# Two transformer blocks on one core: the first layer's modulation sums as one-column matrix products, and its first norm tile by tile

## The chip, the cores and the metric

One core of one Trainium2 chip runs the whole program in a single launch. The metric is device time in microseconds (us); smaller is better. TensorE is called PE, its weight loads PEld, VectorE DVE, ScalarE ACT, GpSimd POOL; SP is the engine that only issues DMAs.

## The reference

A batch of one, 512 tokens of width 1024, fp32. Two layers form a first block, two hybrid layers a second one. The change lies in the first layer of the first block, and there in the adaptive modulation and in the first norm:

```python
s_lat, s_ctx = silu(c), silu(c_ctx)
mod_l = split(s_lat @ ada_w[i] + ada_b[i], 6)      # shift, scale, gate for mixer and for MLP
a_lat = rmsnorm(h_lat, norm1_g[i]) * (1 + mod_l[1]) + mod_l[0]
a_ctx = ...the same for 256 context tokens, with s_ctx...
p_lat = a_lat @ mix_w_in + mix_b_in                # q, k, v and three Hyena streams
kv_ctx = a_ctx @ mix_w_in[:, kv] + mix_b_in[kv]
# differential attention (4 heads, two softmaxes each), a long convolution beside it,
# an output projection, then h_lat + mod_l[2] * y and an MLP with mod_l[3:6]
```

Each of the six modulation vectors of a layer is a vector of 1024 times a 1024 x 1024 matrix. The kernel treats them as twelve halves of 512 columns: halves 0 and 1 are the first shift, 2 and 3 the first scale, 4 to 11 the rest.

## The kernel before

**Products.** Activations lie with channels on the partitions. Every fp32 operand is split into a high part (a rounded copy by ACT) and a low part (source minus high, by DVE or POOL), and a product is three matrix products: high by high, low by high, high by low (`mm3`, lines 458 to 460). A product of 1024 channels is 8 such triples into one of six PSUM banks (`ps`). Two more banks (`pss`) serve everything small: broadcasts, transposes of the attention weights, filter products, statistics.

**The stream of weights.** `plan` writes the order of all weight pieces by hand. Each piece is 512 KB and lands in one of six raw buffers; SP issues the piece that is six later when a buffer's readers are done (`_done_part`). `prefetch` walks ahead of the consumer: high parts for one piece more than low parts. Modulation pieces ("ada") stand between weight pieces and are worked off when the walk passes them. In the first layer the order is: halves 0 and 1 (pieces 0 to 7), q (8), four pieces of k (9 to 12), then pairs of "qh" pieces with two or four ada pieces after each pair.

**Modulation sums before.** A half is four pieces, each 256 rows by 512 columns. `_ada_step` multiplies each row block by its scalar and adds it to an accumulator: in mode `G` by a POOL multiply (line 371) and a POOL add (line 383), in mode `A` by an ACT multiply (line 373) and a POOL add, in mode `V` by one DVE instruction (line 378). A half takes 8 multiplies and 7 adds of 128 x 512. DVE then transposes and reduces the accumulator (lines 416 and 418), and a selection product and a DVE add finish it. The string `ada='GGAGGA'` gives the modes of halves 4 to 9. `first_shift` does the same for halves 0 and 1 with two vectors (latent and context), modes `fs='GGVA'`, and sums over partitions by 32 products with a column of ones (line 1101). `v_shift` sums the shift times the v weights, one accumulator on DVE, one on ACT and POOL (`vs='VA'`).

**The start.** For k from 0 to 7 a strip product (line 1012, 8 products of two columns) gives the scale, `inputs(k)` makes the split operands and the squares, and `groups(k)` runs 18 large products of the v projection. Beside them run the Hyena filter's hidden layer, the first filter taps (line 872) and `first_shift` by the counts in `fstep`. After group 7 the reciprocal root is broadcast by PE (line 563) and copied by ACT to SBUF, the ones products run, then DVE multiplies all eight x tiles (line 1117), and per tile ACT makes the high part, POOL or DVE a full copy (line 1127), DVE or POOL the low part (line 1121). The same follows for the context (lines 1138 to 1141). Then come the projections q, k (four, each also for the context), and 16 attention steps. A step runs the scores (1497, 1498), softmax, one qh projection as filler (`gemm1`), transposes into `pss` (1538), splits of them (1550) and the product with v.

Of the kernel before, what the change touches and what calls it, by code (L numbers as in the profile page):

```python
# [19 lines left out]
T = 512  # L20
TC = 256
# [4 lines left out]
RAW_BUFS = 6  # L26
# [24 lines left out]
def r(t):  # L51
    return t.bitcast(F32R)


class Weights:
# [9 lines left out]


PR = dict(
    l_q='G',
    l_k='V',
    l_qh='V',  # L70
    l_mo='G',
# [29 lines left out]
    ax='VVVGVVVV',  # L101
    al='VGVVVVGV',
    at='GGGGVGGG',
# [32 lines left out]
class Prog:  # L136
    def __init__(self, tc, ctx, a, out, tap=None):
# [21 lines left out]
        self.ada_acc = {}  # L159
        self.ada_late, self.ada_mode = [], "G"  # L160
        self.look = LOOK
        self.l_eng = self.V
        self.cnt = {}
        self.past0 = False
# [94 lines left out]
    def _emit_l(self):  # L259
        p, part = self.parts[self.cur_l]  # L260
        self.cur_l += 1
        kind, extra = part
        if kind == "ada":
            self._ada_step(p, *extra)
            self._done_part(p)
        elif kind == "w":
# [108 lines left out]
    def add_scaled(self, mode, out, x, sc):  # L375

        if mode == "V":
            self.V.scalar_tensor_tensor(out, x, sc, out, op0=ALU.mult, op1=ALU.add)
        else:
            t = self.get()  # L380
            v = t[:, 0:x.shape[-1]]
            self.scaled(mode, v, x, sc)
            self.G.tensor_tensor(out, out, v, op=ALU.add)  # L383
            self.put(t)

    def _ada_step(self, p, layer, half, i):
        raw = p["raw"]
# [547 lines left out]

    def first_shift(self):

        for half in range(2):
            acc = [self.get(), self.get()]
            for i in range(4):  # L940
                p = self.parts[self.cur][0]
                self.cur_h = self.cur_l = self.cur = self.cur + 1
                for kk in range(2):
                    k = 2 * i + kk
                    for c, o in enumerate(acc):
                        sc, w = self.s2[:, k, c:c + 1], p["raw"][:, kk, :]
                        if k == 0:
                            self.scaled(PR["fs"][2 * half + c], o[:], w, sc)
                        else:
                            self.add_scaled(PR["fs"][2 * half + c], o[:], w, sc)  # L950
                self._done_part(p)
                if i == 3:
                    self.first_acc.append(acc)
                yield


    SIDE = [7, 0, 9, 0, 0, 0, 0, 0]
# [2 lines left out]
    def start(self):  # L960
# [38 lines left out]
        cx = [cxt[k // 2][:, k % 2 * TC:(k % 2 + 1) * TC] for k in range(8)]  # L999
        self.conv3_setup()  # L1000
        gg, sh = c.tile([128, 8, 2], F32, name="gg"), c.tile([128, 8, 2], F32, name="sh")
        b1 = c.tile([128, 8], F32, name="b1")
# [3 lines left out]
        hidden, shift, self.first_acc = self.hyena_hidden(z, w1, w2, w3), self.first_shift(), []  # L1006

        def strip(k):

# [52 lines left out]
        for k in range(8):  # L1062
# [19 lines left out]
            if k == 6:  # L1082
# [11 lines left out]
        bp, rc = self.bcast(y[:, 4:6], 2, self.ps_s, "pss"), self.get()  # L1094
        S.copy(rc[:, 0:TC], bp[:, 0:TC])
        ps = self.ps_s.tile([128, 512], F32, tag="pss", name="pss")
        for half, acc in enumerate(self.first_acc):
            for c_, o in enumerate(acc):
                for k in range(4):
                    j = 8 * c_ + 4 * half + k  # L1100
                    PE.matmul(ps[:, j:j + 1], lhsT=o[:, k * 128:(k + 1) * 128], rhs=self.ones[:, 0:1], start=True, stop=True)
            self.put(acc)
        for c_ in range(2):
            V.tensor_tensor(sh[:, :, c_], ps[:, 8 * c_:8 * c_ + 8], self.col("ada_b", 0, 8), op=ALU.add)
        self.vt = []

        def out(i):
            t = self.get()
            S.activation(t[:], pss[i][:], AF.Copy, scale=y[:, i:i + 1])
            self.vt.append(t)  # L1110

        for i in range(2):
            out(i)
        A, AC = [], []
        self.l_eng = G
        for k in range(8):
            self.eng("ax").tensor_tensor(xs[k][:], xs[k][:], rb[:], op=ALU.mult)
        self.prefetch(2)

        def low(t, hl):  # L1120
            self.eng("al").tensor_tensor(r(hl[1])[:], t[:], hl[0][:], op=ALU.subtract)
            self.put(t)

        for k in range(8):
            t, hl = self.get(), self.pair()
            S.activation(r(hl[0])[:], xs[k][:], AF.Identity, scale=gg[:, k, 0:1], bias=sh[:, k, 0:1])
            self.eng("at").tensor_scalar(t[:], xs[k][:], gg[:, k, 0:1], sh[:, k, 0:1], op0=ALU.mult, op1=ALU.add)
            A.append(hl)
            self.put(xs[k])
            low(t, hl)  # L1130
        self.put(rb)
        for i in range(2, 6):
            out(i)
        for _ in range(8 - 2 * len(PR["tapk"])):
            next(self.filt)
        for k in range(8):
            t, p = self.get(), self.get()
            self.eng("cx").tensor_tensor(cx[k], cx[k], rc[:, 0:TC], op=ALU.mult)
            S.activation(r(p)[:, 0:TC], cx[k], AF.Identity, scale=gg[:, k, 1:2], bias=sh[:, k, 1:2])
            self.eng("ct").tensor_scalar(t[:, 0:TC], cx[k], gg[:, k, 1:2], sh[:, k, 1:2], op0=ALU.mult, op1=ALU.add)  # L1140
            self.eng("cl").tensor_tensor(r(p)[:, TC:2 * TC], t[:, 0:TC], p[:, 0:TC], op=ALU.subtract)
            AC.append(p)
            self.put(t)
        self.put(rc)
        self.sh = sh
        self.put(cxt)
        next(self.filt)
        self.vw = vw
        return A, AC

# [48 lines left out]
    def layer0(self):  # L1199
# [10 lines left out]
        def gemm1(label):  # L1210
            return self.gemm1(label, axs)
# [3 lines left out]
        def zq(j, ps):  # L1215
            a = self.rope(ps, bin_(j), rope)
            self.defer(lambda: Q.__setitem__(j, self.stack_put(a, True)), PR["zqd"])

        zq(0, gemm1("q"))
        self.l_eng = V  # L1220
        KL, KC = [], []
        for j in range(4):
            w = self.consume("k")
            ps, pc = self.ps(), self.ps()
            for k in range(8):
                self.mm3(ps[:], w[k], axs[k], k == 0, k == 7)
# [1188 lines left out]
```

## Time and profile before

| | us |
|---|---|
| median of 3 runs | 2660.74 |
| lowest, highest | 2656.87, 2663.26 |
| the profiled execution | 2662.61 |
| its span, first to last instruction | 2660.8 |

Mean granted PE clock 0.955 of full. Busy over the span: PE 2477.6, PEld 2066.3, DVE 1831.9, POOL 1458.0, ACT 1136.4 us. The mixer of the changed layer takes about the first 466 us. An engine's busy time counts the time in which some instruction of it is under way; for PE, ends are modelled, so a busy PE is not a PE at its peak. The time of a wait stands in square brackets in a timeline, with the instruction that ended it.

### The profile page before, as it was taken

How to read it: one execution, taken by the hardware profiler on the slowest of the kernel's cores; microseconds unless marked ns; L12 is line 12 of the kernel's file. 1: busy time of each engine (PE TensorE's matmuls, PEld its weight loads, DVE VectorE, ACT ScalarE, POOL GpSimd, SP SyncE). 2: the span in 40 equal slices, each digit the busy share in tenths (PEclk: the TensorE clock that was granted, in tenths of full speed). 3: DMA queues.
4: the chain of work that ended last, by engine and by line, in shares of the span. 5: the costliest groups of instructions: out<-in, count | busy, mean ns of one | idle time of the engine just before them, and what ended most of it. 6: DMA issues, size and time to landing. Idle time of an engine off the chain costs nothing.

```text
span 2660.8 us, 31920 instructions
## 1 busy us (share of the span) xinstructions
PE 2477.6 (93%) x11472; PEld 2066.3 (78%) x11472; DVE 1831.9 (69%) x2646; ACT 1136.4 (43%) x2105; POOL 1458.0 (55%) x1168
## 2 busy tenths in 40 slices
PE   7787878999989899999879999999999899999998
PEld 6565767887868788888768888888887688888887
DVE  7899987776666787766778677455477876733334
ACT  3446653532233543334567545222256654522231
POOL 6687756399991379963575346878136744100001
PEclk8798888999999999999989999999999899999999
DMA  7233322366664167762212235666332123233321
GB/s 253 73 125 96 118 88 80 97 193 200 197 204 140 48 171 213 218 188 82 89 52 70 72 116 164 184 195 199 111 89 87 44 82 119 81 94 97 101 86 50
DMA packets 433367, 330.29 MB, mean 124 GB/s; under 512 B 11799, under 2 KB 365207, under 8 KB 433208
## 3 DMA queue, kind: packets, MB, share of 16 engines
q1 hardware_dynamic: 429976, 322.22, 40.4%
q0 software_dynamic: 3232, 6.03, 0.7%
q8 instruction: 90, 1.47, 0.2%
q14 instruction: 69, 0.57, 0.1%
HBM read 319.82 MB, written 8.39 MB: 123 GB/s over the span
## 4 chain that ended last, share of the span: by engine, by line
PE 59%; DVE 19%; POOL 11%; ACT 4%; issue 3%; DMA 2%; SPq 0%; POOLq 0%; DVEq 0%; ACTq 0%
PE ps L458 17%; PE ps L459 16%; PE ps L460 16%; POOL slot L383 6%; POOL slot L371 5%; PE ps L619 4%; PE ps L477 3%; DVE slot L273 2%; DVE slot L1988 1%; DVE slot L527 1%; DVE slot L1940 1%; DVE slot L1550 1%; DVE slot L2053 1%; PE pss L574 1%; PE ps L1382 1%
## 5 line engine op out<-in xcount | busy, mean ns | idle before, releaser
L458 PE MATMUL ps<-slot 128*128 128x512 f32 (+1 forms) x3024 | 1168.7, 386 | 56.8 <-DVE slot L527 17.0
L460 PE MATMUL ps<-slot 128*128 128x512 f32 (+1 forms) x3024 | 1159.3, 383 | 20.8 <-DVE slot L527 9.2
L459 PE MATMUL ps<-slot 128*128 128x512 f32 (+1 forms) x3024 | 1161.0, 384 | 18.4 <-DVE slot L273 15.5
L458 PEld LDWEIGHTS ps<-slot 128*128 128x128 f32 x3024 | 583.4, 193 | 171.5 <-DVE slot L527 20.1
L460 PEld LDWEIGHTS ps<-slot 128*128 128x128 f32 x3024 | 582.3, 193 | 132.0 <-DVE slot L527 9.4
L459 PEld LDWEIGHTS ps<-slot 128*128 128x128 f32 x3024 | 583.4, 193 | 126.3 <-DVE slot L273 18.1
L255 ACT CAST slot<-raw 128x512 fp32r<-128x512 f32 (+1 forms) x764 | 425.7, 612 | 345.0 <-DMA raw<-in_mlp_w_dram 219.4
L273 DVE TENSOR_TENSOR slot<-raw,slot 128x512 fp32r<-128x512 f32 x588 | 510.2, 911 | 35.4 <-ACT slot L255 34.1
L383 POOL TENSOR_TENSOR slot<-slot 128x512 f32<-128x512 f32 x336 | 491.3, 1462 | 59.0 <-ACT slot L373 31.6
L542 POOL TENSOR_TENSOR slot<-slot 128x512 f32<-128x512 f32 (+1 forms) x64 | 90.8, 1423 | 585.5 <-ACT slot L536 585.0
L273 POOL TENSOR_TENSOR slot<-raw,slot 128x512 fp32r<-128x512 f32 (+1 forms) x176 | 251.7, 1454 | 175.8 <-ACT slot L255 134.8
L371 POOL TENSOR_SCALAR slot<-raw,cols 128x512 f32<-128x512 f32 x192 | 206.8, 1080 | 110.8 <-DMA raw<-in_w_ada_dram 57.3
L371 POOL TENSOR_SCALAR slot<-raw,s_lat 128x512 f32<-128x512 f32 x144 | 155.7, 1084 | 35.3 <-PE ps L619 19.2
L619 PE MATMUL ps<-slot 128*128 128x512 f32 x576 | 147.5, 416 | 6.0 <-DVE slot L1818 6.0
L2201 DVE TENSOR_TENSOR slot<-slot,ps 128x512 f32<-128x512 f32 x40 | 27.5, 687 | 174.6 <-PE ps L460 174.6
L536 ACT ACTIVATE slot<-slot 128x512 f32<-128x512 f32 (+1 forms) x98 | 55.3, 575 | 214.2 <-DVE slot L1713 60.0
L619 PEld LDWEIGHTS ps<-slot 128*128 128x128 f32 x576 | 115.0, 202 | 31.8 <-DVE slot L1818 7.4
L526 ACT CAST slot<-slot 128x512 fp32r<-128x512 f32 x80 | 47.1, 619 | 183.4 <-DVE slot L2201 155.6
L477 PE MATMUL ps<-slot 128*128 128x512 f32 x480 | 111.1, 390 | 4.1 <-ACT slot L526 2.8
L477 PEld LDWEIGHTS ps<-slot 128*128 128x128 f32 x480 | 89.7, 188 | 23.8 <-ACT slot L526 3.2
L527 DVE TENSOR_TENSOR slot<-slot 128x512 fp32r<-128x512 f32 x75 | 78.1, 1062 | 36.4 <-ACT slot L526 36.4
L2226 DVE SCALAR_TENSOR_TENSOR slot<-ps,mod,slot 128x512 f32<-128x512 f32 x40 | 30.0, 750 | 102.2 <-PE ps L460 102.2
(321 smaller groups left out, 2734.9 us busy)
## 6 DMA issues: line engine op xcount, KB each, us to landing
raw<-in_mlp_w_dram SPq DMA_DIRECT2D x128, 512.0 KB, 4.4
raw<-in_w_ada_dram SPq DMA_DIRECT2D x96, 512.0 KB, 4.4
raw<-in_ada_w_dram SPq DMA_DIRECT2D x88, 512.0 KB, 4.8
raw<-in_w_ffn_in_dram SPq DMA_DIRECT2D x88, 512.0 KB, 4.2
raw<-in_w_in_dram SPq DMA_DIRECT2D x56, 512.0 KB, 3.8
raw<-in_w_ffn_out_dram SPq DMA_DIRECT2D x32, 512.0 KB, 5.2
raw<-in_mix_w_dram SPq DMA_DIRECT2D x20, 512.0 KB, 3.9
raw<-in_w_out_dram SPq DMA_DIRECT2D x16, 512.0 KB, 4.0
```

The lines of the kernel that those rows point to most:

```text
L255: self.S.copy(r(v), src[:, k:k + kk, :])
L273: eng.tensor_tensor(r(lv), src, v, op=ALU.subtract)
L371: self.G.tensor_scalar(out, x, sc, 0.0, op0=ALU.mult, op1=ALU.add)
L383: self.G.tensor_tensor(out, out, v, op=ALU.add)
L458: self.PE.matmul(out, lhsT=wh, rhs=xh, start=start, stop=False)
L459: self.PE.matmul(out, lhsT=wl, rhs=xh, start=False, stop=False)
L460: self.PE.matmul(out, lhsT=wh, rhs=xl, start=False, stop=stop)
L477: self.PE.matmul(ps[:], lhsT=w[k][i], rhs=xs[k][j], start=(k == 0 and n == 0), stop=(k == kc - 1 and n == 2))
L527: (eng or self.V).tensor_tensor(r(l)[:, 0:n], src, h[:, 0:n], op=ALU.subtract)
L536: self.S.activation(sq[:, 0:n], x, AF.Square, scale=scale)
L542: (eng or self.G).tensor_tensor(st["acc"][:, 0:n], st["acc"][:, 0:n], sq[:, 0:n], op=ALU.add)
L619: PE.matmul(ps[:], lhsT=w[i][:, m * 128:(m + 1) * 128], rhs=r(x[j])[:], start=(k == 0 and n == 0), stop=(k == 7 and n == 2))
```

## The change

It touches only the first layer.

- Halves 4 to 7 of the modulation become PE work (`.` in `ada`). `columns` multiplies the raw fp32 weight block (as the stationary operand, 128 x 128) by one column of the vector: 8 products for a piece, two for each of four blocks of outputs, into one `pss` bank; one small DVE add then puts them into the modulation vector. The products are queued as jobs, and `work` strings them between the large ones: two after each triple of a projection, or one after each triple of a context product, the remainder at its end. A piece stays "open" until its job is done, and SP's issues stop five pieces behind the oldest open one. Halves 8 and 9 go to ACT and POOL (half 8 was on POOL alone).
- `first_shift`: half 0 by ACT multiplies and POOL adds; half 1 by PE, two columns at a time. The steps are placed later: `fstep` (1,2,1,0,0,1,0,3) becomes (0,1,1,0,0,2,1,3), so the last three pieces are PE work after group 7.
- `v_shift`: both accumulators on ACT and POOL. The low part of q moves from POOL to DVE.
- The first norm: `prefetch(3)` stands ahead of it, in place of `prefetch(2)` within it. The broadcast is read by DVE straight from PSUM. Per tile: DVE multiply, ACT high part, full copy by DVE for odd and by ACT for even tiles, DVE low part; POOL has no part in it.
- q and the first two k run as three accumulators side by side, tile after tile; three steps of the filter move from the context norm to behind them.

```diff
-    l_q='G',
+    l_q='V',
-    ada='GGAGGA',
-    fs='GGVA',
-    vs='VA',
-    fstep=(1, 2, 1, 0, 0, 1, 0, 3),
+    ada='....AA',
+    fs='AA',
+    vs='AA',
+    fstep=(0, 1, 1, 0, 0, 2, 1, 3),
...
     def _done_part(self, p):
-        self._dma_to(p["idx"] + RAW_BUFS)
+        self.dma_want = max(self.dma_want, p["idx"] + RAW_BUFS)
+        self._dma_to(min([self.dma_want] + [i + RAW_BUFS - 1 for i in self.open]))
...
+    def columns(self, raw, vec, k0, n, done):
+
+        ps = self.ps_s.tile([128, 512], F32, tag="pss", name="pss")
+        for j in range(4):
+            for kk in range(2):
+                self.PE.matmul(ps[:, n * j:n * j + n], lhsT=raw[:, kk, j * 128:(j + 1) * 128],
+                               rhs=vec[:, n * (k0 + kk):n * (k0 + kk) + n], start=(kk == 0), stop=(kk == 1))
+                yield
+        done(ps[:, 0:4 * n])
+
+    def work(self, n=None):
+
+        while self.jobs and n != 0:
+            if next(self.jobs[0], self) is self:
+                self.jobs.pop(0)
+            elif n:
+                n -= 1
+
+    def _ada_columns(self, p, layer, half, i):
+        m, b = self.mod[layer][:, half * 4:half * 4 + 4], self.col("ada_b", layer * 48 + half * 4, 4)
+        self.open.append(p["idx"])
+
+        def done(o):
+            self.V.tensor_tensor(m, o, b if i == 0 else m, op=ALU.add)
...
         for k, x in enumerate(xs):
             self.mm3(ps[:], w[k], x, k == 0, k == len(xs) - 1)
+            self.work(2)
+        self.work()
...
+        for i in range(4):
+            p = self.parts[self.cur][0]
+            self.cur_h = self.cur_l = self.cur = self.cur + 1
+            self.jobs.append(self.columns(p["raw"], s2, 2 * i, 2, lambda x: self.V.tensor_tensor(o, o, x, op=ALU.add)))
+            self.work()
+            self._done_part(p)
+            yield
...
-        bp, rb = self.bcast(y, 4, self.ps_s, "pss"), self.get()
-        S.copy(rb[:], bp[:])
...
+        self.prefetch(3)
...
+        def norm(x, f, n, c_, hi, lo, k):
+
+            t, z = self.get(), self.get()
+            sc, b = gg[:, k, c_:c_ + 1], sh[:, k, c_:c_ + 1]
+            V.tensor_tensor(t[:, 0:n], x, f, op=ALU.mult)
+            S.activation(r(hi), t[:, 0:n], AF.Identity, scale=sc, bias=b)
+            if k % 2:
+                V.tensor_scalar(z[:, 0:n], t[:, 0:n], sc, b, op0=ALU.mult, op1=ALU.add)
+            else:
+                S.activation(z[:, 0:n], t[:, 0:n], AF.Identity, scale=sc, bias=b)
+            V.tensor_tensor(r(lo), z[:, 0:n], hi, op=ALU.subtract)
+            self.put(t, z)
...
-        zq(0, gemm1("q"))
+        look, self.look = self.look, 0
+        ws = [self.consume(n) for n in ("q", "k", "k")]
+        self.look = look
+        pss = [self.ps() for _ in ws]
+        for k in range(8):
+            for w, ps in zip(ws, pss):
+                self.mm3(ps[:], w[k], axs[k], k == 0, k == 7)
+        self.put(ws[0].tiles)
+        zq(0, pss[0])
         self.l_eng = V
         KL, KC = [], []
+        for _ in range(8 - 2 * len(PR["tapk"])):
+            next(self.filt)
+        next(self.filt)
...
+            if j < 2:
+                w, ps, pc = ws[j + 1], pss[j + 1], self.ps()
+                if j == 0:
+                    self.prefetch(self.look)
+            else:
+                w = self.consume("k")
+                ps, pc = self.ps(), self.ps()
+                for k in range(8):
+                    self.mm3(ps[:], w[k], axs[k], k == 0, k == 7)
+                    self.work(2)
             for k in range(8):
                 self.mm3(pc[:, 0:TC], w[k], acs[k], k == 0, k == 7)
+                self.work(1)
+            self.work()
```

## Rows read from the trace of the kernel before

**Rows 1.** Busy us of each engine by stretch, with its length first

```profile
28.00:89.30 61.30, 48.28 (x198) 38.71 (x197) 53.91 (x68) 19.94 (x38) 47.74 (x37) 0.78 0.52 177
89.30:143.00 53.70, 41.29 (x178) 33.00 (x177) 47.12 (x63) 31.82 (x55) 36.29 (x28) 0.78 0.23 69
143.00:320.00 177.00, 138.98 (x637) 114.22 (x636) 167.62 (x243) 98.88 (x216) 138.01 (x110) 0.87 0.36 116
320.00:466.00 146.00, 117.58 (x602) 100.86 (x601) 120.17 (x206) 69.23 (x142) 85.93 (x63) 0.89 0.27 83
466.00:865.00 399.00, 383.70 (x1715) 317.02 (x1714) 272.32 (x345) 137.62 (x239) 289.31 (x235) 0.97 0.57 172
```

**Rows 2.** TensorE by line, 28-89.3 us (count, busy, mean ns, idle before)

```profile
L1012 PE MATMUL pss<-s,slot 128*128 128x2 f32 x60 | 9.4, 262 | 0.0
```

**Rows 3.** TensorE's timeline (start, us): products of few columns, large ones

```profile
19.43 0.95 PE L1012 MATMUL pss<-s,slot 128*128 128x2 f32 x8
...
20.24 0.47 PE L458 MATMUL ps<-slot 128*128 128x512 f32 x1
...
56.47 0.76 PE L458 MATMUL pss<-slot 128*128 128x512 f32 x1 [5.66 <-DVE gg L1017]
...
94.93 3.57 PE L1101 MATMUL pss<-ones,slot 128*128 128x1 f32 x16 [2.42 <-DVE slot L378]
```

**Rows 4.** Timeline of VectorE around the first norm

```profile
88.41 6.47 DVE L378 SCALAR_TENSOR_TENSOR slot<-raw,s,slot 128x512 f32<-128x512 f32 x6
...
106.02 0.68 DVE L1121 TENSOR_TENSOR slot<-slot 128x512 fp32r<-128x512 f32 x1
...
127.16 0.43 DVE L1141 TENSOR_TENSOR slot<-slot 128x256 fp32r<-128x256 f32 x1
```

**Rows 5.** Timeline of the SP queue, one issue

```profile
51.51 11.44 SPq L233 DMA_DIRECT2D raw<-in_mix_w_dram  x2
```

**Rows 6.** POOL by line, 128-466 us

```profile
L383 POOL TENSOR_TENSOR slot<-slot 128x512 f32<-128x512 f32 x49 | 72.3, 1476 | 35.1 <-ACT slot L373 31.6
L371 POOL TENSOR_SCALAR slot<-raw,s_lat 128x512 f32<-128x512 f32 x32 | 32.9, 1030 | 0.0
```

**Rows 7.** VectorE by line, 128-466 us

```profile
L273 DVE TENSOR_TENSOR slot<-raw,slot 128x512 fp32r<-128x512 f32 x40 | 40.1, 1041 | 0.1
...
L378 DVE SCALAR_TENSOR_TENSOR slot<-slot,sh 128x512 f32<-128x512 f32 x7 | 9.6, 1375 | 0.2
...
L416 DVE STREAM_TRANSPOSE slot<-slot 128x512 f32<-128x512 f32 x6 | 4.2, 704 | 0.1
L418 DVE TENSOR_REDUCE ada_r<-slot 128x16 f32<-128x512 f32 x6 | 4.1, 686 | 0.2
```

**Rows 8.** Line 273 on VectorE: 600-730 us, then 2300-2450 us

```profile
L273 DVE TENSOR_TENSOR slot<-raw,slot 128x512 fp32r<-128x512 f32 x43 | 47.9, 1151 | 7.4 <-ACT slot L255 6.2 <-POOL slot L383 1.2
...
L273 DVE TENSOR_TENSOR slot<-raw,slot 128x512 fp32r<-128x512 f32 x58 | 36.8, 686 | 13.9 <-ACT slot L255 13.9
```

**Rows 9.** All engines by line, 0-130 us

```profile
L1023 ACT ACTIVATE slot<-slot,gg 128x512 fp32r<-128x512 f32 x8 | 5.8, 721 | 29.0 <-DVE gg L1017 21.9 <-POOL slot L371 4.0 <-POOL slot L383 3.1
...
L872 DVE TENSOR_TENSOR slot<-pss,slot 128x512 f32<-128x512 f32 x8 | 5.4, 679 | 0.0
...
L1104 DVE TENSOR_TENSOR sh<-pss,cols 128x8 f32<-128x8 f32 x2 | 0.2, 162 | 3.7 <-PE pss L1101 3.7
```

**Rows 10.** Timeline of TensorE and VectorE, attention steps 3 and 7

```profile
223.78 0.40 PE L458 MATMUL ps<-slot 128*128 128x512 f32 x1
...
231.69 0.39 PE L460 MATMUL ps<-slot 128*128 128x256 f32 x1 [2.01 <-DVE slot L1550]
...
230.95 1.28 DVE L1550 TENSOR_TENSOR slot<-pss,slot 128x512 fp32r<-128x512 f32 x2
...
270.84 0.62 PE L458 MATMUL ps<-slot 128*128 128x512 f32 x1
...
277.27 1.28 DVE L1550 TENSOR_TENSOR slot<-pss,slot 128x512 fp32r<-128x512 f32 x2
```

More of the change, by code (lines that the diff above doesn't have):

```diff
@@ L384, in add_scaled @@
             self.put(t)
+    def columns(self, raw, vec, k0, n, done):
[17 more added lines that the diff above has]
+            self.V.tensor_tensor(m, o, b if i == 0 else m, op=ALU.add)
+            if i == 3:
+                self.ready.add((layer, half))
+            self.open.remove(p["idx"])
+            self._done_part(p)
+        self.jobs.append(self.columns(p["raw"], self.s_lat, 2 * i, 1, done))
     def _ada_step(self, p, layer, half, i):
@@ L936, in first_shift @@
     def first_shift(self):
[L938 to L954, printed above, removed]
+        acc, s2 = [self.get(), self.get()], self.s2[:].rearrange("p k c -> p (k c)")
+        self.first_acc = acc
+        for i in range(4):
+            p = self.parts[self.cur][0]
+            self.cur_h = self.cur_l = self.cur = self.cur + 1
+            for kk in range(2):
+                k = 2 * i + kk
+                for c, o in enumerate(acc):
+                    sc, w = self.s2[:, k, c:c + 1], p["raw"][:, kk, :]
+                    if k == 0:
+                        self.scaled(PR["fs"][c], o[:], w, sc)
+                    else:
+                        self.add_scaled(PR["fs"][c], o[:], w, sc)
+            self._done_part(p)
+            yield
+        o = self.sh[:, 4:8, :].rearrange("p k c -> p (k c)")
+        for c in range(2):
+            self.V.tensor_copy(self.sh[:, 4:8, c], self.col("ada_b", 4, 4))
+        for i in range(4):
+            p = self.parts[self.cur][0]
+            self.cur_h = self.cur_l = self.cur = self.cur + 1
+            self.jobs.append(self.columns(p["raw"], s2, 2 * i, 2, lambda x: self.V.tensor_tensor(o, o, x, op=ALU.add)))
+            self.work()
+            self._done_part(p)
+            yield
     SIDE = [7, 0, 9, 0, 0, 0, 0, 0]
@@ L1091, in start @@
                     next(self.filt)
-        bp, rb = self.bcast(y, 4, self.ps_s, "pss"), self.get()
-        S.copy(rb[:], bp[:])
-        bp, rc = self.bcast(y[:, 4:6], 2, self.ps_s, "pss"), self.get()
-        S.copy(rc[:, 0:TC], bp[:, 0:TC])
+        self.prefetch(3)
         ps = self.ps_s.tile([128, 512], F32, tag="pss", name="pss")
[L1097 to L1102, printed above, removed]
+        for c_, o in enumerate(self.first_acc):
+            for k in range(4):
+                j = 4 * c_ + k
+                PE.matmul(ps[:, j:j + 1], lhsT=o[:, k * 128:(k + 1) * 128], rhs=self.ones[:, 0:1], start=True, stop=True)
+        self.put(self.first_acc)
         for c_ in range(2):
-            V.tensor_tensor(sh[:, :, c_], ps[:, 8 * c_:8 * c_ + 8], self.col("ada_b", 0, 8), op=ALU.add)
+            V.tensor_tensor(sh[:, 0:4, c_], ps[:, 4 * c_:4 * c_ + 4], self.col("ada_b", 0, 4), op=ALU.add)
         self.vt = []
@@ L1112, in start @@
+        A, AC = [], []
+        bp = self.bcast(y, 4, self.ps_s, "pss")
         for i in range(2):
             out(i)
-        A, AC = [], []
-        self.l_eng = G
         for k in range(8):
[L1117 to L1127, printed above, removed]
+            hl = self.pair()
+            norm(xs[k][:], bp[:], T, 0, hl[0][:], hl[1][:], k)
@@ L1128, in start @@
             A.append(hl)
             self.put(xs[k])
-            low(t, hl)
-        self.put(rb)
-        for i in range(2, 6):
+            if k in (2, 4):
+                out(1 + k // 2)
+        bp = self.bcast(y[:, 4:6], 2, self.ps_s, "pss")
+        for i in range(4, 6):
             out(i)
-        for _ in range(8 - 2 * len(PR["tapk"])):
-            next(self.filt)
         for k in range(8):
[L1137 to L1141, printed above, removed]
+            p = self.get()
+            norm(cx[k], bp[:, 0:TC], TC, 1, p[:, 0:TC], p[:, TC:2 * TC], k)
```

17 lines of the change are left out of this document (7 added, 10 removed).

## Prediction

> **What bounds the kernel now.** I read the busy time by stretch first [rows 1]. From 466 us on PE is the bound (383.7 busy of 399). Before that it is not: PE is busy 139 of 177 us in the attention steps (143 to 320), while DVE is busy 167.6 of 177 and POOL 138. The mixer of the first layer is therefore paced by DVE, and PE's clock shows it: 0.78 of full in both stretches of the start, 0.87 in attention, 0.97 behind. The change moves work only ahead of 466 us; what it gains there shifts everything behind, and what it loses too.
>
> The start has slack of its own. Between 28 and 89.3 us PE runs 198 products, of which 60 have two columns [rows 1, 2]. At full clock a large product starts 0.224 us after another (383.7 / 1715 in the PE-bound stretch [rows 1]) and eight two-column ones take 20.24 - 19.43 = 0.81 us, 0.10 each [rows 3]. So the stretch holds 138 x 0.224 + 60 x 0.10 = 37 us of PE work in 61.3 us. The other 24 us are waits and half clock: for example a wait of 5.66 us for DVE at 56.47, behind which a large product took 0.76 us instead of 0.47 [rows 3]. POOL is busy 47.7 of these 61.3 us [rows 1], mostly with the first shift's sums.
>
> The third view is VectorE by line. The same instruction, line 273, takes 0.686 us where POOL does nothing (2300 to 2450 us) and 1.151 us where POOL is nearly always at work [rows 8]; in the mixer it takes 1.041 us [rows 7]. An instruction with one PSUM operand, line 872, keeps 0.679 us beside a busy POOL [rows 9]. So POOL's work costs DVE time, the engine that is the bound.
>
> **Start, up to the end of group 7: -10 us.** The first shift's POOL work falls from 16 multiplies and 21 adds to 14 adds, and eight of these come only after group 5. DVE loses one multiply and seven fused adds of line 378; six of those stood at 88.41 for 6.47 us on the path to the norm [rows 4]. ACT takes 16 multiplies at 0.72 us, the price of line 1023 [rows 9], 11.5 us on an engine busy 20 of 61 us. On SP, the q piece was issued in a wait of 11.44 us from 51.51 [rows 5], in front of the filter tables; q now waits for a buffer that ACT frees after group 5, and the tables' issue passes it. PE gains eight two-column products in group 6 (0.8 us). The bounds are 0 (the waits have other causes too: filter taps, DMA) and the whole 24 us. I take 10, somewhat under half, because waits for DVE that POOL slows are only one part of the 24.
>
> **From group 7 to the end of the first norm: 0.** Before, the first low part stood at 106.02, 16.7 us behind group 7, and the last context tile at 127.16 [rows 4]. After: 24 two-column products and eight ones products (32 x 0.10 to 0.22 [rows 3], so 3 to 7 us), which take the place of 32 ones products. ACT must also cast the third piece of k, whose raw buffer comes free only with those products, and is in order; with the DMA, casts, outputs, high part, copy and low part I estimate the first low part 10 us behind group 7, about 7 earlier than before. Then comes a chain that is not pipelined: on an even tile DVE's multiply (0.68), ACT's high part and copy (0.72 and about 0.6 behind it), DVE's low part (0.69), on an odd tile about 2.1; a pair takes 4.8 us, four pairs 19, the context tiles about 14. DVE so ends its norm some 40 us behind group 7, against 38 before, and three filter steps (about 3.5 us of DVE) still stand behind it that were inside before. On PE, q and two k's need 72 large products (16 us), which hide beneath the tiles, so PE is ahead by one k (24 x 0.224 = 5.4 us). Taken together 0, between -9 (PE's lead counts in full) and +8 (DVE's lag and the half clock count).
>
> **Attention and what follows, to 466 us: -7.** What DVE loses: seven adds of line 378 and their multiply, 10 us; four of six transposes and reductions, (4.2 + 4.1) x 4/6 = 5.5 us [rows 7]. What it gains: 16 small adds at 0.16, the price of line 1104 [rows 9], 2.6 us. POOL loses 32 multiplies and 28 of the 49 adds, and gets back 7 in `v_shift`: 32.9 + 21 x 1.476 = 64 us of the 224 between 143 and 466 [rows 1, 6]. That frees DVE a second time. Line 273 alone runs 40 instructions that lie 0.355 us over the undisturbed 0.686 us, 14.2 us [rows 7, 8]; 64 of 224 us of that gives 4 us as the lower bound. For the upper one, each of the 53 removed POOL instructions costs a DVE instruction the full difference of 0.465 us [rows 8], 25 us. I take 15, as many other instructions with two SBUF operands are slowed too. DVE's relief is thus 10 + 5.5 - 2.6 + 15 = 28 us.
>
> The Trainium skill's page "SBUF — State Buffer", section "SBUF: two separate sides", says that this port pair is an exclusive lock: a DVE instruction with two SBUF inputs and a POOL instruction exclude each other for a whole instruction. By that, up to all 64 us could come back to DVE. Row 273 agrees in sign, but its 1.151 us is less than one full POOL add more, so I keep the sum from the rows.
>
> What PE pays: 128 one-column products, 12.8 us at full clock (0.10 each), 28 at the half-level price (3.57 / 16 = 0.22) [rows 3]. And waits. The products need a `pss` bank, and there are two. In the steps 3, 5 and 7 the transposes hold both until DVE has made the low parts. In step 3 the filler projection started at 223.78 and ran without a wait up to 231.69, because only the product with v needed those parts (it waited 2.01 us); DVE split the banks at 230.95 [rows 10]. Now the first column stands behind the first triple, at about 224.5, and would wait until DVE is through the first bank at about 231.6, 7 us. In step 7 the filler starts at 270.84 and DVE splits the banks at 277.27 [rows 10], so 6 us; step 5 I take as short of a wait. The present waits in front of the product with v, some 3 us, vanish in exchange. So PE gets 12.8 + 10 = 23 us more, beside 38 us in which it idles now between 143 and 320 [rows 1]. The gain is DVE's 28 us less what PE's blocked lead starves DVE of; if some 21 of the 23 us show, 7 are left, between -28 (all of PE's part hidden) and +14 (the columns at their half-level price of 28 us, and only half of the relief of use).
>
> ACT's eight multiplies for `v_shift` and eight for half 8 against eight fewer for half 6 are free at a load of 99 of 177 us; without that cover they would cost 6 us. The small DVE adds hold DVE until PE has reached them, which is in the waits above. From 466 us on nothing changes, and POOL's sums there stay.
>
> **Sum.** Profiled execution 2662.6 (span 2660.8 and 1.8 around it): -10 + 0 - 7 = -17, 2645.6. The median of the runs is 1.9 lower than that execution, so 2643.7, rounded 2644.
>
> **Rivals.**
> - *As summed* (0.47): 2644, own range 2630 to 2655.
> - *The relief counts in full* (0.22). The start gives 22 of its 24 us, and DVE's faster instructions end ahead of the `pss` waits, so attention gives 25: 2660.7 - 47 = 2614. For it: DVE at 95% there. Against it: PE's 139 + 23 already fills 162 of the 177 us. The exclusive lock of the Trainium skill's page above speaks for this rival.
> - *No change* (0.14). The gains of the start are absorbed by the unpipelined norm (+8), and attention is neutral: 2660.7 - 10 + 8 = 2659.
> - *Slower: column products tie PE to DVE's queue through two banks* (0.17). Place: the k projection with 32 columns, and steps 3, 5 and 7. Besides 23 us, a wait of 5.66 us left PE at the half level for some products [rows 3], about 1.4 us for each of three such waits, and the third and fourth piece of two projections wait for the first piece's add, say 3 us each. With the 6 us more that step 5 can take when DVE is late there, that makes 33 to 35 us on PE; it decides once more than DVE's 28 us of it fall on steps in which DVE has nothing else queued. If it lands in full, with 5 us of the start gained and 10 of the relief usable: 2660.7 + 35 - 15 - 8 (hidden in waits that stay) = 2673. For it speaks the late split of the banks [rows 10]. Against it: DVE reaches those splits earlier. The Trainium skill's page "TensorE: Matmul & The Clock Gate", section "A second HAM failure mode: psum-queue depth-cycling", tells of just such short idles between banks lowering the clock; the row at 56.47 agrees for a wait of 5.66 us [rows 3].
>
> Faster by over 0.2% (5.3 us, about what runs of this kernel can tell from none) then has 0.69, within it 0.14, slower 0.17. The range 2612 to 2668 leaves out about half of the slower case and the lower part of the second.
>
> **What would show it.** Right: line 378 gone ahead of the norm, group 7 ending near 79 us, line 273 in the mixer near 0.9 us, POOL 64 us lighter, columns of about 0.10 us. Wrong if PE waits of over 5 us on `pss` stand in front of columns in steps 3, 5, 7 and DVE idles behind them, or if group 7 still ends near 89.

## The result, and the profile of the changed kernel

The changed kernel takes 2692.99 us (median of four runs, 2689.13 to 2697.15), against 2660.07 for the kernel before (also four runs): a ratio of 1.0124 with a 95% interval of 1.0104 to 1.0144. It is 33 us slower, where 2644 was forecast, and outside the range.

The first view is again the busy time by stretch, with the same edges as [rows 1] (stretch; busy us and count of PE, PEld, DVE, ACT, POOL; PE clock; DMA share; GB/s):

```profile
28.00:89.30 61.30, 54.26 (x279) 46.79 (x278) 45.76 (x75) 30.64 (x56) 24.06 (x18) 0.84 0.58 193
89.30:143.00 53.70, 40.85 (x156) 33.95 (x156) 37.52 (x69) 28.30 (x46) 6.27 (x4) 0.66 0.19 58
143.00:320.00 177.00, 156.58 (x701) 136.52 (x701) 104.76 (x186) 83.67 (x176) 58.85 (x45) 0.74 0.26 84
320.00:466.00 146.00, 116.62 (x580) 99.93 (x579) 118.16 (x215) 76.20 (x165) 74.66 (x59) 0.84 0.32 101
466.00:865.00 399.00, 381.01 (x1712) 315.77 (x1711) 273.71 (x341) 139.65 (x242) 307.98 (x247) 0.98 0.56 171
```

In attention (143 to 320) everything has turned round. DVE, the bound before with 167.6 busy of 177, is busy 104.8; POOL fell from 138 to 59; and PE, which had 38 us to spare, is busy 156.6, at a mean clock of 0.74 in place of 0.87. A part of this is the fixed window, which holds less of the work when everything comes later. From the first scores to the last (the score products of the first and the last attention step), DVE is busy 138.0 of 216.0 us, before 174.5 of 192.8.

The place of the loss follows from landmarks of the two PE timelines. Group 7 ends at 79.5 in place of 89.3: ten us earlier, as forecast. The first scores start at 195.07 in place of 177.79, 17 later; the last scores at 411.07 in place of 370.64, 40 later; the output projection at 444.92 in place of 404.50. Some 6 us come back behind that, and the span is 34.6 longer. So all is lost between group 7 and the last scores.

The second view is the list of waits in 143 to 466 us (who waits for whom; us in total, times, longest), first DVE's, then PE's:

```profile
DVE mod L413 <- PE pss L395: 53.8, 10, 8.4
DVE mx L1555 <- PE ps L1554: 18.9, 8, 4.5
...
PE pss L395 <- issue: 12.5, 3, 8.1
...
PE pss L395 <- DVE mod L413: 6.9, 1, 6.9
...
PE pss L395 <- DVE slot L1205: 1.0, 1, 1.0
```

DVE stands 53.8 us in ten small adds (L413), each time for a column product. No such line exists before. In return the columns (L395) wait 6.9 us for such an add, and 12.5 us "for issue", which the next view names. These three lines of PE add up to 20.4 us, and 20.4 is all that PE idles between 143 and 320: it waits there for no weight piece and for no softmax, only in front of columns. So PE is the bound, and SP's held-back issues are not the cause there. The third view is PE's timeline in the third attention step (start, us, instruction; in brackets the wait before it):

```profile
231.80 0.39 PE L495 MATMUL ps<-slot 128*128 128x512 f32 x1
240.25 0.98 PE L395 MATMUL pss<-s_lat,raw 128*128 128x1 f32 x4 [8.07 <-issue]
241.09 0.77 PE L493 MATMUL ps<-slot 128*128 128x512 f32 x1
241.67 0.63 PE L494 MATMUL ps<-slot 128*128 128x512 f32 x1
242.09 0.63 PE L495 MATMUL ps<-slot 128*128 128x512 f32 x1
...
244.65 0.85 PE L395 MATMUL pss<-s_lat,raw 128*128 128x1 f32 x4
...
246.79 0.85 PE L395 MATMUL pss<-s_lat,raw 128*128 128x1 f32 x4
...
255.32 7.67 PE L395 MATMUL pss<-s_lat,raw 128*128 128x1 f32 x36
262.86 0.56 PE L493 MATMUL ps<-slot 128*128 128x256 f32 x1
```

and DVE's in the same step:

```profile
239.47 1.28 DVE L1607 TENSOR_TENSOR slot<-pss,slot 128x512 fp32r<-128x512 f32 x2
...
247.67 0.16 DVE L413 TENSOR_TENSOR mod<-pss,cols 128x4 f32<-128x4 f32 x1 [2.30 <-PE pss L395]
256.20 0.16 DVE L413 TENSOR_TENSOR mod<-pss,mod 128x4 f32<-128x4 f32 x1 [8.37 <-PE pss L395]
259.62 0.16 DVE L413 TENSOR_TENSOR mod<-pss,mod 128x4 f32<-128x4 f32 x1 [3.25 <-PE pss L395]
```

Three things are seen. The columns start 8.07 us after the first triple, as soon as the first of the two splits that begin at 239.47 (L1607) is through: this is the wait for a bank that the prediction put at 7 us. Then a large triple with its four column instructions takes 2.13 us (244.65 to 246.79), up to 255.32, and the 36 that are left take 7.54 us in a row: 22.6 us with PE busy throughout, at the half level of its clock (large products start 0.43 us apart, at the full level 0.23). And DVE, in order, stands in the adds. The same period at the full level, earlier in the same trace, is 1.14 us:

```profile
160.44 0.50 PE L395 MATMUL pss<-s_lat,raw 128*128 128x1 f32 x4
160.80 0.47 PE L493 MATMUL ps<-slot 128*128 128x512 f32 x1
161.12 0.39 PE L494 MATMUL ps<-slot 128*128 128x512 f32 x1
161.34 0.40 PE L495 MATMUL ps<-slot 128*128 128x512 f32 x1
161.58 0.50 PE L395 MATMUL pss<-s_lat,raw 128*128 128x1 f32 x4
```

Last, the groups by line in 128 to 466 us, which answer to [rows 6, 7] and to the price of a column (busy us, mean ns):

```profile
L395 PE MATMUL pss<-s_lat,raw 128*128 128x1 f32 x256 | 50.8, 307 | 21.2 <-issue 12.5 <-DVE mod L413 6.9 <-DVE slot L1205 1.0
...
L387 POOL TENSOR_TENSOR slot<-slot 128x512 f32<-128x512 f32 x28 | 39.6, 1431 | 56.4 <-ACT slot L377 55.6
...
L277 DVE TENSOR_TENSOR slot<-raw,slot 128x512 fp32r<-128x512 f32 x34 | 26.0, 807 | 0.1
```

There are 256 column instructions for 128 products: an fp32 product is issued as two. The relief came: the multiplies of L375 no longer stand in this stretch and 28 adds are left, and L277 (L273 before) takes 0.807 us instead of 1.041. It was not used.

### The profile page after: what moved, and what is told of

Same layout as the page of the kernel before. It is cut to its first block, busy times and chain, and to the rows that moved or that the text cites. A ratio compares the mean times of both kernels' runs of the same rounds, so it can differ in the third digit from the quotient of the medians.

```text
span 2695.4 us, 32463 instructions
## 1 busy us (share of the span) xinstructions
PE 2531.8 (94%) x11776; PEld 2125.1 (79%) x11776; DVE 1774.4 (66%) x2658; ACT 1153.0 (43%) x2127; POOL 1341.2 (50%) x1070
## 4 chain that ended last, share of the span: by engine, by line
PE 67%; DVE 14%; POOL 10%; ACT 4%; issue 3%; DMA 2%; SPq 0%; POOLq 0%; DVEq 0%; ACTq 0%
PE ps L493 18%; PE ps L494 18%; PE ps L495 18%; POOL slot L387 5%; POOL slot L375 4%; PE ps L656 4%; PE ps L512 3%; PE pss L395 2%; DVE slot L2045 1%; DVE slot L1997 1%; DVE slot L277 1%; DVE slot L564 1%; PE pss L611 1%; DVE slot L2110 1%; PE ps L1439 1%
## 5 line engine op out<-in xcount | busy, mean ns | idle before, releaser
L277 DVE TENSOR_TENSOR slot<-raw,slot 128x512 fp32r<-128x512 f32 x590 | 501.4, 894 | 37.0 <-ACT slot L257 34.6
L387 POOL TENSOR_TENSOR slot<-slot 128x512 f32<-128x512 f32 x308 | 450.0, 1464 | 92.1 <-ACT slot L377 69.1
L277 POOL TENSOR_TENSOR slot<-raw,slot 128x512 fp32r<-128x512 f32 (+1 forms) x174 | 250.4, 1463 | 172.2 <-ACT slot L257 132.1
L375 POOL TENSOR_SCALAR slot<-raw,cols 128x512 f32<-128x512 f32 x192 | 207.0, 1081 | 110.9 <-DMA raw<-in_w_ada_dram 57.2
L375 POOL TENSOR_SCALAR slot<-raw,s_lat 128x512 f32<-128x512 f32 x112 | 123.1, 1102 | 31.4 <-PE ps L656 17.0
```

The costliest lines, as they stand in the source:

```text
L277: eng.tensor_tensor(r(lv), src, v, op=ALU.subtract)
L375: self.G.tensor_scalar(out, x, sc, 0.0, op0=ALU.mult, op1=ALU.add)
```

## The experiments

All ratios are to the kernel before, run beside each kernel. Its median beside the experiments was 2656.2 to 2659.7, so that medians of different rows compare less well than ratios. Each kernel ran 4 to 10 times. First and last scores are from the one profiled run of each.

| kernel | median us | ratio, 95% interval | first scores | last scores |
|---|---|---|---|---|
| before | 2660.07 | 1 | 177.8 | 370.6 |
| changed | 2692.99 | 1.0124 (1.0104 to 1.0144) | 195.1 | 411.1 |
| sums back | 2658.59 | 1.0013 (1.0003 to 1.0022) | 178.9 | 372.1 |
| columns alone | 2694.68 | 1.0144 (1.0129 to 1.0159) | 187.4 | 405.8 |
| block behind | 2659.46 | 1.0011 (1.0000 to 1.0023) | 186.7 | 368.7 |
| start alone | 2655.61 | 0.9998 (0.9988 to 1.0008) | 171.0 | 368.1 |
| block ahead | 2686.87 | 1.0111 (1.0096 to 1.0127) | 193.6 | 401.6 |
| strung late | 2666.29 | 1.0033 (1.0020 to 1.0046) | 188.9 | 378.5 |
| 64 columns | 2661.47 | 1.0015 (1.0006 to 1.0025) | 185.4 | 374.6 |
| start and block | 2651.42 | 0.9982 (0.9969 to 0.9995) | 178.8 | 362.8 |
| 64 columns, late | 2661.77 | 1.0011 (1.0002 to 1.0021) | 188.4 | 373.5 |
| start, block, 64 columns | 2649.98 | 0.9972 (0.9961 to 0.9983) | 179.5 | 363.8 |
| other banks | 2664.35 | 1.0026 (1.0011 to 1.0040) | 181.9 | 376.8 |
| adds off DVE | 2685.93 | 1.0101 (1.0088 to 1.0114) | 181.4 | 400.0 |
| start, block, 64 columns, adds off DVE | 2643.73 | 0.9939 (0.9927 to 0.9951) | 173.5 | 354.7 |

### Which part loses: sums back, columns alone, start alone

Sums back, from the changed kernel:

```diff
-    ada='....AA',
+    ada='GGAGGA',
```

> The changed kernel, but halves 4 to 9 are summed as before (ada='GGAGGA'); the shift, the norm and the order q, k, k stay changed. Theory A (the one-column products of halves 4 to 7 make the loss of 33 us: two instructions each, so 256 x 0.10 = 26 us of PE at full clock, the half clock around them, and waits for the two small PSUM banks): 2645 to 2660. Rival B (the unpipelined norm and the order q, k, k make it): above 2680.

Columns alone: the kernel before with `columns`, `work` and `_ada_columns` of the change, and

```diff
-    ada='GGAGGA',
+    ada='....GA',
```

> The kernel before, with halves 4 to 7 alone as strung one-column products (ada='....GA'); shift, norm and order as before. Theory A: 2690 to 2705. Rival B: 2655 to 2665.

Start alone: the kernel before with the new `first_shift` and `v_shift` (`fs='AA'`, `vs='AA'`, the new `fstep`), its own norm, order and sums.

> The kernel before with the changed first shift and v shift (fs, fstep, vs; half 1 as two-column products), the old norm, the old order and the old sums of halves 4 to 9. Theory A: 2645 to 2660, within 6 us of the run with the sums back. Rival B: 20 us or more below that run.

Without the strung columns the loss is gone (1.0013), and alone they make all of it (1.0144). Norm and order are not the cause. They aren't free either: sums back and start alone differ in norm, order and the engine of q's low part, and the first scores come at 178.9 against 171.0, 8 us later; by the end of the norm 4 of these are there (the last context tile stands at 126.60 against 122.84). Start alone has its first scores 6.8 us earlier than the kernel before, but the last only 2.5 earlier, and ends where it did.

### Price of the products, or where they stand: block behind, block ahead, strung late

Block behind (the changed kernel; the same in the loops of k):

```diff
             self.mm3(ps[:], w[k], x, k == 0, k == len(xs) - 1)
-            self.work(2)
         self.work()
```

> The changed kernel, with the same one-column products, but all of a projection's in one block behind its 24 large ones, none between them. If stringing them (PE stays at half clock among them) and the early wait for a bank are the main cost: 2665 to 2680. If their own price is: 2688 to 2698. Rival B: 2690 to 2696, as the norm is untouched.

The same 128 products, behind a projection's large ones, cost nothing on balance: by the ratios, 30 us are back, more than the expectation allowed, and the kernel stands where sums back stands. So the price of a product, though twice what I took, is no more than the relief of DVE pays for; the loss lies where the products stand. Two theories were left: the half level that strung columns hold (H), and the wait of the first column for a bank (W).

Block ahead moves `self.work()` to the front of a projection; strung late keeps the string, `self.work(4 if k > 3 else 0)`, and 2 in place of 4 behind a context product.

> The changed kernel with all waiting column products of a projection in one block ahead of its 24 large products, none between them. The block asks for its bank of pss even earlier than the strung columns do. Theory H (the strung columns cost by the half level that they hold PE at): 2655 to 2668, as nothing is strung. Theory W (the cost is PE standing in front of the first column until DVE has split the scores and frees a bank, and DVE then starving): at or above 2680, with waits of 5 us and more in front of the columns.

> The changed kernel with the same columns strung, but only between the last four large triples of a projection, four products behind each. The first column comes about 3 us later, so more of the waits for a bank are over by then. Theory H: still strung, so the half level stays; 2680 to 2692. Theory W: the waits shrink by about 3 us each; 2660 to 2672.

Both came out as theory W had it. But the trace of block ahead shows that it is not W alone:

```profile
237.99 13.78 PE L395 MATMUL pss<-s_lat,raw 128*128 128x1 f32 x64 [8.92 <-issue]
251.64 0.77 PE L493 MATMUL ps<-slot 128*128 128x512 f32 x1
```

Behind the wait of 8.92 us, 64 column instructions took 13.65 us (237.99 to 251.64), 0.213 each: the half level, with nothing large between them. The theories could not be told apart by order.

### The clock and the banks, each by itself: 64 columns, other banks

64 columns (the order and the banks of the changed kernel):

```diff
         ps = self.ps_s.tile([128, 512], F32, tag="pss", name="pss")
+        wide = n == 1
+        m, rhs = (64, self.cols) if wide else (n, vec)
         for j in range(4):
             for kk in range(2):
-                self.PE.matmul(ps[:, n * j:n * j + n], lhsT=raw[:, kk, j * 128:(j + 1) * 128],
-                               rhs=vec[:, n * (k0 + kk):n * (k0 + kk) + n], start=(kk == 0), stop=(kk == 1))
+                self.PE.matmul(ps[:, m * j:m * j + m], lhsT=raw[:, kk, j * 128:(j + 1) * 128],
+                               rhs=rhs[:, 0:m] if wide else rhs[:, n * (k0 + kk):n * (k0 + kk) + n], start=(kk == 0), stop=(kk == 1))
```

> The changed kernel with 64 columns instead of one in each strung product of the modulation sums: the moving operand is another tile, so the four values added to a sum are other numbers, and everything else stands. Same order, same waits for banks, more work on PE by 128 products. Theory H, in the form that what lowers the clock is how little a one-column product gives PE to do: the granted clock of the strung stretches rises, and the time falls below that of the changed kernel, to 2665 to 2688, though PE has more to do. Theory H, in the form that the alternation itself (a weight load in fp32 between large products) lowers it, or theory W: at or above 2693, with the clock as low as in the changed kernel.

By the ratios it gave 29 us back; 2661.47 is below what the theory was given. In this order the forecast of theory H's first form came, and the other two did not. It is not general, as both cures together will show. The timeline at the place shown above:

```profile
228.03 1.09 PE L397 MATMUL pss<-cols,raw 128*128 128x64 f32 x4 [8.60 <-issue]
...
230.31 0.95 PE L397 MATMUL pss<-cols,raw 128*128 128x64 f32 x4
...
232.44 0.95 PE L397 MATMUL pss<-cols,raw 128*128 128x64 f32 x4
...
234.14 0.55 PE L397 MATMUL pss<-cols,raw 128*128 128x64 f32 x4
235.28 0.55 PE L397 MATMUL pss<-cols,raw 128*128 128x64 f32 x4
...
242.64 0.36 PE L495 MATMUL ps<-slot 128*128 128x256 f32 x1
```

The same wait for a bank stands there, 8.60 us, and the string begins at the half level, 2.13 us a period (230.31 to 232.44); but from 234.14 the period is 1.14, and the projection is through after 14.6 us (228.03 to 242.64) where one column needed 22.6 (240.25 to 262.86). At the full level 64 columns cost PE what one does, 1.14 us a period in both; at the half level too, 2.13. Busy time and clock of this kernel, 143 to 320 us, and then its list of waits, 143 to 466 us:

```profile
143.00:320.00 177.00, 152.15 (x838) 131.38 (x837) 128.07 (x236) 101.92 (x221) 73.49 (x56) 0.92 0.35 111
```

```profile
DVE mod L415 <- PE pss L397: 27.8, 10, 6.2
```

The clock is 0.92 in place of 0.74, and DVE's wait in the adds half of what it was.

Other banks (the changed kernel, one column):

```diff
-        ps = self.ps_s.tile([128, 512], F32, tag="pss", name="pss")
+        ps = self.ps() if n == 1 else self.ps_s.tile([128, 512], F32, tag="pss", name="pss")
```

> The changed kernel, strung one-column products as they were, but their sums lie in the six banks of ps in place of the two of pss, so that no column waits for DVE's split of the scores; a projection then has one bank fewer. Theory H: the clock stays at the half level in the strung stretches, 2675 to 2693. Theory W: the wait of 8.1 us at 240 and those of 6.9, 3.1 and 1.4 us are gone and with them most of the loss, 2655 to 2670.

2664.35: as theory W had it, 26 us back. The waits in front of the columns shrink to between 1.2 and 1.6 us, and the clock is 0.86: more of the strings of one-column products begin and stay at the full level. PE's timeline, then the busy time of the stretch:

```profile
192.60 0.50 PE L395 MATMUL ps<-s_lat,raw 128*128 128x1 f32 x4
...
193.75 0.50 PE L395 MATMUL ps<-s_lat,raw 128*128 128x1 f32 x4
```

```profile
143.00:320.00 177.00, 166.38 (x850) 145.00 (x850) 125.87 (x234) 103.33 (x222) 71.78 (x55) 0.86 0.35 108
```

Other strings of this run stand at the half level, that of the third step too, which still takes 21.8 us (215.17 to 236.97; in the changed kernel 22.6). So neither theory is the whole: each cure alone takes back nearly all.

Why one is enough can be worked out from the traces. I add up the strings behind 143 us, each from its first column to the product behind its last one, and the wait in front. They took PE 106 us in the changed kernel, 81 with 64 columns and 74 with other banks. At the full level and without waits they would take about 52, an estimate from 0.227 us a large product, 0.12 one of 256 columns and 0.115 a column instruction. So the excess is 54, 29 and 22 us. The cures save PE 25 and 32 us, and they save the kernel 29 and 26. What PE saves the kernel saves, about; and what is left of the excess costs little (4 and 7 us), as PE had time to spare: it idled 38 us in attention before. This account fits, but no run varies the slack by itself. Both cures together:

> The changed kernel with both cures: each modulation product gets its one column read 64 times over as the moving operand (64 equal columns come out, the first is added), and the products are strung only between the last four large triples of a projection. If the half level and the early wait for a bank are the whole loss and add: the one cure alone gave 2661.5, the other 2666.3, the changed kernel 2693; by the sum of both gains 2635, by the overlap of both (each alone regains most of the same stretches) 2650 to 2660. I expect 2653.

The edit reads the one column 64 times over (`v.to_broadcast([128, 64])`) and strings late. 2661.77, above all that was expected: the gains do not add. Most of them could not, as sums back and block behind, which have no strings, are no faster by their ratios. And at the longest string the 64 columns did nothing here:

```profile
228.78 1.94 PE L397 MATMUL pss<-s_lat,raw 128*128 128x64 f32 x8 [5.90 <-issue]
...
237.88 8.63 PE L397 MATMUL pss<-s_lat,raw 128*128 128x64 f32 x40
246.26 0.56 PE L495 MATMUL ps<-slot 128*128 128x256 f32 x1
```

PE is at the half level for all of these 17.48 us (228.78 to 246.26). Strung late, with one column, has the same 17.48 us at this place (229.41 to 246.89), behind the same wait of 5.90. So that a string has one column is not by itself what holds it at the half level.

### Who carries PE's lateness: adds off DVE

```diff
-            self.V.tensor_tensor(m, o, b if i == 0 else m, op=ALU.add)
+            t = self.small(4, "cs")
+            self.S.copy(t[:], o)
+            self.G.tensor_tensor(m, t[:], b if i == 0 else m, op=ALU.add)
```

> The changed kernel; only the small add that takes a piece's four sums out of PSUM is moved off DVE: ACT copies them to SBUF and POOL adds them. Products, banks and order are as they were. Theory D (the loss reaches the chain because DVE, in order, stands in these small adds for PE, 55 us in 11 waits): 2655 to 2670. Theory P (PE's own lateness behind half level and bank is what counts, whoever reads the sums): 2680 to 2695. The copy may hold ACT as the add held DVE; then the wait shows on ACT in the list of waits, and the time lies with theory P.

2685.93, in the range of theory P. In attention the wait moved to ACT, as the expectation's last sentence allowed, and DVE now stands in front of the scores instead. The list of waits, 143 to 466 us, ACT's and DVE's:

```profile
ACT cs L414 <- PE pss L395: 56.2, 11, 8.4
...
DVE mx L1557 <- PE ps L1556: 64.4, 9, 21.8
```

From the first scores to the last it takes 218.6 us, in the changed kernel 216.0: there DVE's in-order queue, which I had named as the link, is not what makes the loss. PE stands still for 14.4 us between 143 and 320, nearly all in front of columns again. But ACT works in order too, so this clears DVE's queue and not that of every engine that reads the sums.

Ahead of the first scores DVE's queue does count. In the k projection of the changed kernel a column waits 6.93 us for a DVE add, and the string behind it is at the half level; with the adds on ACT the wait is gone and the string stays at the full level. First the changed kernel, then adds off DVE:

```profile
175.17 0.59 PE L395 MATMUL pss<-s_lat,raw 128*128 128x1 f32 x2 [6.93 <-DVE mod L413]
```

```profile
167.76 0.38 PE L395 MATMUL pss<-s_lat,raw 128*128 128x1 f32 x2 [0.20 <-ACT cs L414]
```

The first scores come 13.7 us earlier (181.4 against 195.1), the last 11; by the ratios some 6 us of that reach the end, not clear of the noise.

### Towards a faster version

> The kernel before with the new first shift, and with the columns of four modulation halves in a block behind the large products of a projection; norm and order of the projections are those of the kernel before. The start alone had its first scores 6.8 us earlier than before (171.0 against 177.8 us), and the block alone went from the first scores to the last in 182 us against 193. If both gains add: some 17 us earlier at the last scores, 2638 to 2645. If the columns ahead of the first scores cost what they cost in the block alone (first scores at 186.7 us): 2650 to 2660.

> The kernel before with the new first shift, columns in a block behind a projection's large products (2651.4 with one column), and each product with its one column read 64 times over. In the one-column form the blocks of 64, 42 and 24 instructions took 10.26, 9.04 and 5.26 us where they would take about 7.3, 4.8 and 2.8 at the full level. If one column is what holds PE at the half level: these 9.7 us come back, 2640 to 2646. If the block of fp32 products is too short to show it, or DVE sets the pace again: 2648 to 2653.

> The kernel of the best run (old order, new first shift, 64 equal columns in a block, 2650.0), with the small adds on ACT and POOL too. DVE waited 15.5 us there in such adds. If DVE's wait is still worth something: 2640 to 2647. If PE is early enough in this order: 2648 to 2653.

Start and block gained 0.18%, less than the additive 17 us: the columns ahead of the first scores cost 7.8 of the start's gain (178.8 against 171.0), while attention went in 184 us. 64 columns in blocks gave 1 to 3 us (by medians, by ratios), within the noise, and the time lies in the second case of the expectation: the block of 64 instructions at 219 us took 13.41 us (219.98 to 233.39) where one column had 13.60 (219.30 to 232.90), both at the half level. (The blocks of 42 and 24 instructions in the expectation are two views of this one block.) With the adds on ACT and POOL as well, the kernel takes 2643.73, 0.61% under the kernel before (interval 0.49% to 0.73%), and is the fastest of all. The small adds did cost something here too: 15.5 us of DVE's waits, and 6 to 9 us of the end, about what adds off DVE gave in the strung order.

## Why the prediction was wrong, point by point

- **Start, -10 us: right in place and size, worthless in the end.** Group 7 ended ten us earlier. Start alone shows that nothing of it reaches the end: attention, paced by DVE, takes 197 us instead of 193 from the first scores to the last. Why is not shown; `v_shift` on ACT and POOL is one candidate that was not tried by itself.
- **Group 7 to the norm's end, 0: mis-sized.** It cost 8 us, the upper bound that was given for it. The last context tile stood 37.9 us behind group 7 before (127.16 [rows 4]) and stands 46.2 behind it now, so that at this point 1.4 of the ten us are left:

```profile
79.53 1.84 PE L395 MATMUL pss<-s,raw 128*128 128x2 f32 x16
81.66 5.79 PE L395 MATMUL pss<-s,raw 128*128 128x2 f32 x32 [0.28 <-DVE slot L909]
87.31 3.55 PE L1143 MATMUL pss<-ones,slot 128*128 128x1 f32 x16
```

```profile
125.74 0.43 DVE L1164 TENSOR_TENSOR slot<-slot 128x256 fp32r<-128x256 f32 x1 [0.22 <-ACT slot L1159]
```

The 24 two-column and eight ones products are 64 instructions. They took 11.2 us (79.53 to 90.72) in place of 3 to 7, and the first low part came 14.6 us behind group 7 (94.13) in place of 10. The 32 products of line 1101 before are likewise 16, in 32 instructions.
- **Attention, the DVE part (28 us of relief): right, if anything low.** In block behind, which has the same sums, DVE is busy 134.0 and 117.2 us in the two stretches where it was 167.6 and 120.2 [rows 1]: 36.6 less. From the first scores to the last it is busy 139.8 us there, 174.5 before, and this stretch took 182 us instead of 193. L277 came out at 0.807 us where about 0.9 was the sign given.
- **Attention, "What PE pays": the step that failed.** The stretch from the first scores to the last was to get shorter and took 216 us instead of 193. The price of a product was read from eight instructions as eight products; 256 instructions for 128 products make it 0.23 us at the full level ((1.14 - 3 x 0.227) / 2, with 0.227 as the distance of large products alone) and 0.43 at the half level, not 0.10 and 0.22. The half level was put on the columns alone (28 us as an upper bound); in truth the large products strung between them fall with it, and they are the larger part of 1 us a period. And "some 21 of the 23 us show" was reckoned against DVE's relief, as though DVE stayed the bound; PE became it. What PE paid behind 143 us was not 23 us but 54 (the excess worked out above), and the price of the products at the full level besides.
- **Ahead of the first scores** the sum has no wait at all, but the changed kernel comes there 16 us behind sums back (195.1 against 178.9). The wait of 6.93 us for an add stands there, in the k projection. Only the fourth rival had it.
- **The wait for a bank** was forecast in the right place and size: 7 us in step 3, and 8.07 came. In steps 5 and 7 it was 1.4 and 3.1 us, for a short one and 6. The sign of being wrong came true in step 3: a wait of over 5 us in front of columns, DVE idle behind it. It was treated as a term that only adds its own length. In the changed kernel more follows: PE comes out of it at the half level, and stays there for the whole string.
- **The fourth rival** (slower, 2673, 0.17) had the mechanism nearest to the truth, columns tied to two banks and half clock behind waits. It fell short by 20 us, and put the clock at 1.4 us a wait, where the step shown lost 8 us (22.6 against 14.6). Its own terms (23, three times 1.4, 3 for each of two projections, 6) add up to some 39 us, not 33 to 35, which would have made it 2677.
- **The clock gate.** The prediction cited the Trainium skill's page "TensorE: Matmul & The Clock Gate", section "A second HAM failure mode: psum-queue depth-cycling", for short idles between banks that lower the clock. Other banks agrees in direction: the waits in front of the columns are 1.2 to 1.6 us there in place of up to 8.1, and the mean clock is 0.86 against 0.74.

What stays open: why one string falls to the half level and another, with the same instructions, does not. In other banks the string at 215.17 fell, behind a wait of 1.56 us, and that at 253.25 did not, behind 1.44.

## What to carry to other kernels

An engine's slack is not a store into which work of any kind can be put: count the new work at the half level too, with everything strung between it, and if the sum then passes the slack, the engine is the new bound. Put small products where their bank is free and their reader is not in a hurry, in a block behind the large ones. And if several single cures each take back nearly the whole loss, look for slack: each may only have to bring the new bound back below the old one, and then their gains do not add.

## What the runs showed of the hardware

- An fp32 product with a 128 x 128 stationary block is two instructions in these traces (256 for 128 products), together 0.23 us at the full level and about 0.43 at the half level, with 1 column or with 64.
- PE was busy without a gap and stayed at the half level for over 20 us (240.25 to 262.86 of the changed kernel) with one-column products between the large ones and in a row behind them, and for 17.5 us with 64 columns (228.78 to 246.26 of 64 columns, late). Other strings of one-column products stand at the full level from end to end (159.30 to 167.64 of the changed kernel). Plain large products of the same trace, begun at the half level at 187.07, take 0.63 us each up to 191.51 and 0.39 from 192.31; the string of 64 columns, begun there at 228.03, is at the full level from 234.14.
- Moving an add of 4 columns from one in-order engine to another moved its wait: 53.8 us on DVE, 56.2 on ACT.
- The same DVE instruction with two SBUF operands (L273, L277) took 1.041 us where POOL was busy 230 of 338 us (128 to 466) and 0.807 where it was busy 139.
